# Sums of log decays over chunks as 64-row blocks in the two row halves of the TensorE array

## The chip, the cores and the metric

The kernel runs on one core of a Trainium2 chip. The metric is the device time of one execution in microseconds (us). The time before the change is 1380.78 us, the median of three runs (1379.42 to 1381.92).

## The reference

Two layers of a trunk with four parallel branches run over 128 context tokens and 512 latent tokens. One branch is an RWKV-7 mixer with a forward and a backward scan, and its decays are what the change touches:

```python
wd_t = jnp.tanh(wd.astype(jnp.float32))
for d, rev in ((0, False), (1, True)):
    w_log = -jax.nn.softplus(-(lp['rw_w0'][d] + wd_t @ lp['rw_w_up'][d])) - 0.5
    decay = heads(jnp.exp(-jnp.exp(w_log)))
    ...
    s_fin, o = wkv_scan(s_init[:, d], r_h, decay, k_d, v_h, kk, a, rev)
```

Inside the scan every step computes `S = S * w_t - sa * (kk_t * a_t) + v_t * k_t` and reads out `S r_t`. The other branches are a chunk mixer, an attention (windowed for the latent tokens) and a pooling mixer; all are gated, projected up, merged and projected out.

## The kernel before

All 640 tokens (T) are held as columns, in two halves of 320 (HF). The large products are taken with 128x128 weights from HBM, each split into a high and a low part in a reduced fp32 format, so that a product is three matmuls over 320 columns: `hi,whi`, `lo,whi`, `hi,wlo`, written to a PSUM tile `m`. These are called mains here. They come in a fixed order and run almost without a break.

Everything else is side work, in Python generators that the class `Clock` weaves between the mains. `Clock` keeps a table of modelled costs and times, and at each `yield` of the main stream it decides whether a side generator's next step is issued. So the order of the instructions on all engines is settled when the program is written, and a change in one step's shape can move later steps. The matmuls of a step stand together, as an island between mains. Small results go to two PSUM banks `x` that are handed out in turn by `X()`; a step that takes a bank waits until its earlier contents have been read.

The scan of the mixer works on chunks of 64 tokens (C; NC = 10 of them) with plain fp32 matmuls, which the trace shows as two records each. `scan(ft, ...)` runs once for each half of the features (ft 0 and 1), and in it `decay(d)` once for each direction, in both layers: eight times in all. `decay` has three steps. The first makes the rates `th` and `kd`; the second computes `s1`, the log decays, as 128 tokens by 128 features in five tiles; the third sums `s1` along each chunk. For the sum `s1[:, tt, :]` (128 tokens, so two chunks) is the stationary operand, loaded as weights, and the constant `tri0` or `tri1` (128x128) is the moving one. `tri0` is zero outside its two diagonal blocks of 64, and `tri1` outside its two off-diagonal ones, so that a token meets only its own chunk (in `tri1` the two chunks change places, as the backward scan runs from the end). The sums go through two exponentials on ScalarE, to `w` and `wi`, which `keys(d)` multiplies into `kb` and `qr` on VectorE.

In the trace `s1`, `w` and `wi` are parts of a tile named A, the constants are `cst`, and the matmuls of the third step read `x<-cst,A`. In the attention of the latent tokens, `x<-xm` and `c<-y,xm` are matmuls; `x<-qr,kb` belongs to the scan and `x<-cst,xm` is a transpose of the chunk mixer. All matmuls have line 332, all transposes line 336, all ScalarE, VectorE and GpSimd work line 291, where helpers issue them.

Of the kernel before, what the change touches and what calls it, by code (L numbers as in the profile page):

```python
# [11 lines left out]
AF = mybir.ActivationFunctionType  # L12
ALU = mybir.AluOpType

P = 128
# [5 lines left out]
T = TP + TS  # L21
HF = T // 2
C = 64
NC = T // C
DECAY = -0.5 * math.exp(-0.5)
# [271 lines left out]
def hybrid_layers_kernel(ctx: ExitStack, tc: tile.TileContext, xt, cond, condb, wm, wt, wa, wb, wo, pa, pb, pc, gfin, kctx, vctx,  # L297
# [16 lines left out]
    def X():  # L314
        return ck.alloc("x", ps_x.tile([P, 512], F32, tag="x", name="x"), 2)
# [8 lines left out]
    V, A, G, PE = Engine(nc.vector, "V", ck), Engine(nc.scalar, "A", ck), Engine(nc.gpsimd, "G", ck), nc.tensor  # L324
# [5 lines left out]
    def mm(out, lhsT, rhs, start=True, stop=True):  # L330
        ck.matmul(out, lhsT, rhs, 1 if rhs.dtype == F32R else 4)
        PE.matmul(out, lhsT, rhs, start=start, stop=stop)  # L332
# [8 lines left out]
    def K(n):  # L341
        o = CST_AT[n]
        return c_sb[:, o:o + (2 if n == "sel" else P)]
# [330 lines left out]
    def layer(l, h, prb):  # L674
# [23 lines left out]
        def scan(ft, ta, kt, rt, vt):  # L698
            kk, th = ta[:, 1], ta[:, 3]
            tb = S([P, 4, T], "A1")  # L700
            kd, w, wi, s1f = (tb[:, i] for i in range(4))
            s1 = s1f.rearrange("p (n c) -> p n c", c=P)
# [7 lines left out]
            def decay(d):  # L710
                pxs = [X(), X()]
                for b, px in enumerate(pxs):
                    mm(px[:, 0:HF], ap[ROWS[b], d, ft * P:(ft + 1) * P], adt[ROWS[b], hs[b]])
                for b, px in enumerate(pxs):
                    A.activation(th[:, hs[b]], px[:, 0:HF], AF.Tanh, bias=a0h[:, 2 * d + ft:2 * d + ft + 1], scale=0.5)
                    A.activation(kd[:, hs[b]], th[:, hs[b]], AF.Identity, bias=kab[:, ft:ft + 1],
                                 scale=kah[:, ft:ft + 1])
                    A.activation(th[:, hs[b]], th[:, hs[b]], AF.Identity, bias=eps[:, 3:4], scale=0.5)
                yield
                for t0, n in ((0, 4), (4, 1)):  # L720
                    px = X()
                    for i in range(n):
                        tt = t0 + i
                        mm(px[:, P * i:P * i + P], wdt[0:65, tt * P:(tt + 1) * P], wup[0:65, ft, d])
                    A.activation(s1[:, t0:t0 + n], px[:, 0:P * n].rearrange("p (n c) -> p n c", n=n), AF.Tanh, scale=0.5)
                    V.tensor_scalar(s1[:, t0:t0 + n], s1[:, t0:t0 + n], 1.0, None, ALU.add)
                yield
                for t0, n in ((0, 1), (1, 4)):
                    px = X()
                    for i in range(n):  # L730
                        tt = t0 + i if d == 0 else t0 + n - 1 - i
                        mm(px[:, i * P:(i + 1) * P], s1[:, tt, :], K(f"tri{d}"))
                    sl = slice(t0 * P, (t0 + n) * P)
                    if d:
                        sl = slice(T - (t0 + n) * P, T - t0 * P)
                    A.activation(w[:, sl], px[:, 0:n * P], AF.Exp, scale=DECAY)
                    A.activation(wi[:, sl], px[:, 0:n * P], AF.Exp, scale=-DECAY)

            def keys(d):
                dn = slice(NC * d, NC * d + NC)  # L740
# [20 lines left out]
                else:  # L761
                    V.tensor_tensor(bon, bon, kd, ALU.add)
                    V.scalar_tensor_tensor(bon, bon, prm("rk")[:, ft:ft + 1], rt, ALU.mult, ALU.mult)

            yield from decay(0)
            yield f"{L}k{ft}"
            n2 = []
# [7 lines left out]
            for b in range(2):  # L775
                px = X()
# [12 lines left out]
            for d in range(2):  # L789
                for c0, n in ((0, 8), (8, 2)):  # L790
                    px = X()
                    for hh in range(2):
                        r = slice(64 * hh, 64 * hh + 64)
                        if d:
                            mm(px[r, 0:n * C], K("anti")[r, r], vn[hh][r, c0:c0 + n, :].rearrange("p c s -> p (c s)"))
                            continue
                        for i in range(n):
                            mm(px[r, i * C:(i + 1) * C], vt[r, (c0 + i) * C:(c0 + i + 1) * C], K("ident")[r, r])
                    for hh in range(2):
                        r = slice(64 * hh, 64 * hh + 64)  # L800
                        src = px[r, 0:n * C].rearrange("p (c s) -> p c s", s=C)
                        o0 = 2 * NC - c0 - n if d else c0
                        A.copy(vn[hh][r, o0:o0 + n, :], src[:, ::-1, :] if d else src)
                yield
                yield from keys(d)
                if d == 0:
                    yield from decay(1)
                    yield
            yield
            for b in range(2):  # L810
                px = X()
# [6 lines left out]
            for c0 in range(0, 2 * NC, 4):  # L818
                px = [X(), X()]
                for i in range(4):  # L820
                    for hh in range(2):
                        r = slice(64 * hh, 64 * hh + 64)
# [13 lines left out]
            for c0 in range(0, 2 * NC, 4):  # L836
                px = X()
# [39 lines left out]
            px = [X(), X()]  # L877
# [10 lines left out]
            px = [X(), X()]  # L888
# [805 lines left out]
```

## Time and profile before

| | |
|---|---|
| median of 3 runs | 1380.78 us |
| the profiled execution, its own time | 1381.1 us |
| its span, first to last instruction | 1379.3 us |
| granted TensorE clock, mean | 0.995 |
| TensorE matmuls busy | 1339.5 us (97%) |
| VectorE busy | 926.0 us (67%) |
| ScalarE busy | 565.7 us (41%) |

The time outside the span is 1.8 us. Busy time is the union of the records of an engine. A matmul's record lasts longer than the interval to the next one, because matmuls are pipelined; what a matmul costs is read from start to start.

### The profile page before, as it was taken

What the parts mean: (1) busy time and instruction counts of PE and PEld (TensorE: products, weight loads), DVE (VectorE), ACT (ScalarE), POOL (GpSimd) and SP (SyncE); (2) the same over time, 40 slices, a digit from 0 to 9 for tenths busy, and PEclk for the clock granted to TensorE, in tenths of its full rate; (3) what the DMA queues carried; (4) which work ended last, traced back from release to release, by engine and by line L of the source; (5) the groups of instructions that cost most, each with busy time, mean ns of one, the idle gap of its engine ahead of it and who ended that gap; (6) DMA issues with size and microseconds to landing.
All of it is one profiled execution on the core that took longest, in us unless ns stands there. A gap on an engine that the chain in (4) does not pass through costs nothing.

```text
span 1379.3 us, 27713 instructions
## 1 busy us (share of the span) xinstructions
PE 1339.5 (97%) x11350; PEld 1253.4 (91%) x11350; DVE 926.0 (67%) x2056; ACT 565.7 (41%) x1258; POOL 51.8 (4%) x43
## 2 busy tenths in 40 slices
PE   5999999999999999999999999999999999999997
PEld 3898889988999988999989988899899999899997
DVE  5767778755777865658887767694378585463475
ACT  5456532234532333325554555223354233242364
POOL 0100010000000000000001001100001000000000
PEclk9999999999999999999999999999999999999998
DMA  9421134421224342741223121423122333144012
GB/s 373 142 84 39 62 94 123 108 76 58 68 73 130 108 105 62 259 177 63 76 78 118 62 70 59 106 84 82 32 67 59 89 85 89 38 153 155 22 39 77
DMA packets 86504, 132.61 MB, mean 96 GB/s; under 512 B 44744, under 2 KB 46152, under 8 KB 84456
## 3 DMA queue, kind: packets, MB, share of 16 engines
q1 hardware_dynamic: 86376, 130.84, 30.6%
q8 instruction: 89, 1.46, 0.4%
q14 instruction: 39, 0.32, 0.1%
HBM read 120.46 MB, written 10.35 MB: 95 GB/s over the span
## 4 chain that ended last, share of the span: by engine, by line
PE 83%; issue 6%; DVE 5%; ACT 3%; DMA 1%; POOL 1%; SPq 0%; POOLq 0%; DVEq 0%; ACTq 0%
PE m L332 65%; PE x L332 9%; PE c L332 5%; PE o L332 2%; DVE wlo L291 2%; DVE t L291 1%; ACT whi L291 1%; PE x L336 1%; DMA qr<-wm 1%; PE o L336 1%; DMA xm<-xt 1%; PE c L336 0%; ACT vn L291 0%; DVE kb L291 0%; ACT hi L291 0%
## 5 line engine op out<-in xcount | busy, mean ns | idle before, releaser
L332 PE MATMUL m<-hi,whi 128*128 128x320 f32 x2064 | 664.5, 322 | 3.1 <-ACT whi L291 1.6
L332 PE MATMUL m<-hi,wlo 128*128 128x320 f32 x2064 | 638.7, 309 | 2.8 <-DVE wlo L291 2.8
L332 PE MATMUL m<-lo,whi 128*128 128x320 f32 x2064 | 637.8, 309 | 2.0 <-DVE lo L291 1.3
L332 PEld LDWEIGHTS m<-hi,whi 128*128 128x128 f32 x2064 | 387.7, 188 | 25.6 <-issue 9.9
L332 PEld LDWEIGHTS m<-lo,whi 128*128 128x128 f32 x2064 | 388.2, 188 | 5.1 <-DVE lo L291 2.0
L332 PEld LDWEIGHTS m<-hi,wlo 128*128 128x128 f32 x2064 | 387.6, 188 | 5.6 <-DVE wlo L291 5.6
L291 ACT CAST whi<-raw 128x640 fp32r<-128x640 f32 (+1 forms) x220 | 148.9, 681 | 264.1 <-PE m L332 247.1
L291 DVE TENSOR_TENSOR wlo<-raw,whi 128x640 fp32r<-128x640 f32 (+1 forms) x220 | 171.8, 784 | 106.2 <-ACT whi L291 102.4
L291 ACT ACTIVATE t<-m 128x320 f32<-128x320 f32 x152 | 64.6, 436 | 91.8 <-PE m L332 91.6
L291 DVE SCALAR_TENSOR_TENSOR t<-t,m 128x320 f32<-128x320 f32 x120 | 57.9, 482 | 53.6 <-PE m L332 44.0
L291 DVE TENSOR_TENSOR kb<-kb 80x31 f32<-80x31 f32 (+15 forms) x248 | 84.7, 342 | 11.3 <-DMA kb<-ad 4.6
L332 PE MATMUL m<-ysh,whi 128*128 128x320 f32 x256 | 82.5, 322 | 0.0
L332 PE MATMUL m<-ysh,wlo 128*128 128x320 f32 x256 | 79.1, 309 | 0.0
L332 PE MATMUL m<-ysl,whi 128*128 128x320 f32 x256 | 78.9, 308 | 0.0
L291 DVE CUSTOM_DVE_ANT_0 junk<-wt,sil 128x1024 bf16<-128x1024 f32 x64 | 77.9, 1217 | 0.8 <-DMA wt<-wt 0.8
L291 DVE TENSOR_TENSOR xm<-xm,t 128x320 f32<-128x320 f32 x96 | 49.6, 517 | 3.3
L332 PEld LDWEIGHTS m<-ysh,whi 128*128 128x128 f32 x256 | 48.1, 188 | 2.5 <-issue 0.6
L332 PEld LDWEIGHTS m<-ysl,whi 128*128 128x128 f32 x256 | 48.1, 188 | 0.1
L332 PEld LDWEIGHTS m<-ysh,wlo 128*128 128x128 f32 x256 | 48.1, 188 | 0.0
L291 ACT ACTIVATE vn<-c 64x128 f32<-64x128 f32 x40 | 10.9, 272 | 85.7 <-DVE vn L291 85.7
L291 DVE RECIPROCAL t<-t 128x320 f32<-128x320 f32 x16 | 34.4, 2149 | 10.9 <-ACT t L291 10.9
L291 DVE CUSTOM_DVE_ANT_0 kbt<-x,xm 128x512 f32<-128x512 f32 (+3 forms) x56 | 26.8, 516 | 19.7 <-PE x L332 19.7
(242 smaller groups left out, 1512.4 us busy)
## 6 DMA issues: line engine op xcount, KB each, us to landing
raw<-wb SPq DMA_DIRECT2D x128, 320.0 KB
raw<-wa SPq DMA_DIRECT2D x92, 256.0 KB
wt<-wt SPq DMA_DIRECT2D x32, 512.0 KB
A<-wm SPq DMA_DIRECT2D x4, 1024.0 KB
A<-wo SPq DMA_DIRECT2D x8, 512.0 KB
xm<-xt SPq DMA_DIRECT2D x4, 640.0 KB
ad<-A SPq DMA_DIRECT2D x8, 320.0 KB
qr<-wm SPq DMA_DIRECT2D x2, 1024.0 KB
```

What stands on the lines that cost most here:

```text
L291: return f(out, *a, **k)
L332: PE.matmul(out, lhsT, rhs, start=start, stop=stop)
L336: PE.transpose(out, in_, K("ident"))
```

## The change

The third step of `decay` takes each half of 64 tokens by itself. Matmuls `(tt, rb)` use rows 0 to 63 (rb 0) or 64 to 127 (rb 1) of `s1[:, tt, :]` and only the 64x64 block of `tri` that is not zero. So ten matmuls with 64 rows, 128 weight columns and 64 moving columns stand where five with 128, 128 and 128 stood. They alternate between the row halves. The two halves write to different banks: one bank collects the even chunks, the other the odd ones, five blocks of 64 columns each. Both banks are taken at the start. The four exponentials cover 320 columns each (one bank, five blocks), written to every other block of 64 in `w` or `wi`; before, two covered 128 columns and two 512, and the first pair needed only the first matmul.

```diff
-                for t0, n in ((0, 1), (1, 4)):
-                    px = X()
-                    for i in range(n):
-                        tt = t0 + i if d == 0 else t0 + n - 1 - i
-                        mm(px[:, i * P:(i + 1) * P], s1[:, tt, :], K(f"tri{d}"))
-                    sl = slice(t0 * P, (t0 + n) * P)
-                    if d:
-                        sl = slice(T - (t0 + n) * P, T - t0 * P)
-                    A.activation(w[:, sl], px[:, 0:n * P], AF.Exp, scale=DECAY)
-                    A.activation(wi[:, sl], px[:, 0:n * P], AF.Exp, scale=-DECAY)
+                px = [X(), X()]
+                for tt in range(NC // 2):
+                    for rb in range(2):
+                        r = slice(C * rb, C * rb + C)
+                        n, blk = (4 - tt, 1 - rb) if d else (tt, rb)
+                        mm(px[blk][:, n * C:n * C + C], s1[r, tt, :], K(f"tri{d}")[r, C * blk:C * blk + C])
+                for x, scale in ((w, DECAY), (wi, -DECAY)):
+                    for blk in range(2):
+                        A.activation(x.rearrange("p (n b c) -> p b n c", b=2, c=C)[:, blk],
+                                     px[blk][:, 0:HF].rearrange("p (n c) -> p n c", c=C), AF.Exp, scale=scale)
```

What stands on TensorE at the first of the eight sums (layer 0, ft 0, forward), before:

```order
L332 MATMUL m<-hi_250,whi 128x320
L332 MATMUL m<-lo_251,whi 128x320
L332 MATMUL m<-hi_250,wlo 128x320
L332 MATMUL x<-cst,A_870 128x128 x5
L332 MATMUL m<-hi_248,whi 128x320
L332 MATMUL m<-lo_249,whi 128x320
L332 MATMUL m<-hi_248,wlo 128x320
```

The same place after:

```order
L332 MATMUL m<-hi_250,whi 128x320
L332 MATMUL m<-lo_251,whi 128x320
L332 MATMUL m<-hi_250,wlo 128x320
L332 MATMUL x<-cst,A_870 128x64 x10
L332 MATMUL m<-hi_248,whi 128x320
L332 MATMUL m<-lo_249,whi 128x320
L332 MATMUL m<-hi_248,wlo 128x320
```

Here nothing moves: ten smaller matmuls stand between the same mains. From here on the order of the side work differs in places. The next island, `x<-xm`, follows after 12 mains where it followed after nine; in the scan of layer 0, ft 0, later islands stand some 20 to 60 mains further back, and from its end on the two kernels run much alike. The islands between mains are 269 where they were 271.

One such place is the first transpose of the chunk mixer's values in layer 0 (`x<-cst,xm`), which takes both banks `x`. Before, it follows transposes of `kb`:

```order
L332 MATMUL m<-hi_248,whi 128x320
L332 MATMUL m<-lo_249,whi 128x320
L332 MATMUL m<-hi_248,wlo 128x320
L336 MATMUL x<-cst,kb 128x128 x4
L336 MATMUL x<-cst,xm_2090 128x128 x5
L332 MATMUL m<-hi_250,whi 128x320
```

After, it stands directly behind the fourth of the five `x<-qr,kb` islands, which fill both banks:

```order
L332 MATMUL m<-hi_250,whi 128x320
L332 MATMUL m<-lo_251,whi 128x320
L332 MATMUL m<-hi_250,wlo 128x320
L332 MATMUL x<-qr,kb 128x128 x8
L336 MATMUL x<-cst,xm_2059 128x128 x5
L332 MATMUL m<-hi_248,whi 128x320
```

In layer 1 the two stand so in both kernels.

## Rows read from the trace of the kernel before

**Rows 1.** The page: TensorE's line of part 1, shares of the chain (part 4).

```profile
PE 1339.5 (97%) x11350; PEld 1253.4 (91%) x11350; DVE 926.0 (67%) x2056; ACT 565.7 (41%) x1258; POOL 51.8 (4%) x43
...
PE 83%; issue 6%; DVE 5%; ACT 3%; DMA 1%; POOL 1%; SPq 0%; POOLq 0%; DVEq 0%; ACTq 0%
```

**Rows 2.** Waits of TensorE: total us, times, longest us.

```profile
PE m L332 <- DVE wlo L291: 2.8, 8, 1.0
PE x L336 <- DVE bon L291: 1.7, 1, 1.7
```

**Rows 3.** Timeline of TensorE at the first sum: start, us to the last end.

```profile
92.16 0.31 PE L332 MATMUL m<-lo,whi 128*128 128x320 f32 x1
92.30 0.31 PE L332 MATMUL m<-hi,wlo 128*128 128x320 f32 x1
92.45 1.27 PE L332 MATMUL x<-cst,A 128*128 128x128 f32 x10
93.48 0.39 PE L332 MATMUL m<-hi,whi 128*128 128x320 f32 x1
93.71 0.31 PE L332 MATMUL m<-lo,whi 128*128 128x320 f32 x1
93.85 0.31 PE L332 MATMUL m<-hi,wlo 128*128 128x320 f32 x1
```

**Rows 4.** Timeline at the first of the islands `x<-qr,kb` (64 rows each).

```profile
179.36 0.31 PE L332 MATMUL m<-hi,wlo 128*128 128x320 f32 x1
179.59 1.16 PE L332 MATMUL x<-qr,kb 64*128 64x128 f32 x16
180.69 0.41 PE L332 MATMUL m<-hi,whi 128*128 128x320 f32 x1
180.94 0.31 PE L332 MATMUL m<-lo,whi 128*128 128x320 f32 x1
```

**Rows 5.** Timeline where two moving columns meet 128 weight columns.

```profile
671.19 0.72 PE L332 MATMUL x<-cst,nacc 128*128 128x2 f32 x6
671.78 0.81 PE L332 MATMUL x<-cst,t 128*128 128x2 f32 x6
672.45 0.39 PE L332 MATMUL m<-hi,whi 128*128 128x320 f32 x1
```

**Rows 6.** Timeline where 64 moving columns meet 64 weight columns, in pairs.

```profile
284.09 0.69 PE L332 MATMUL c<-vn,kbt 128*64 128x64 f32 x16 [0.25 <-ACT vn L291]
284.60 0.64 PE L332 MATMUL o<-A,vn 128*64 128x64 f32 x16
```

**Rows 7.** Weight loads grouped by form: count, busy us, mean ns, idle before.

```profile
L332 PEld LDWEIGHTS x<-qr,kb 64*128 64x128 f32 x320 | 19.4, 187 | 3.9 <-issue 2.1 <-DVE t L291 0.6 <-DVE xm L291 0.4
...
L332 PEld LDWEIGHTS c<-vn,kbt 128*64 128x64 f32 x288 | 10.7, 137 | 7.5 <-ACT vn L291 3.9 <-issue 3.1 <-ACT t L291 0.6
...
L332 PEld LDWEIGHTS x<-cst,A 128*128 128x128 f32 x80 | 9.8, 191 | 0.2 <-DVE mp L291 0.2
```

**Rows 8.** ScalarE grouped by form: count, busy us, mean ns, idle before.

```profile
L291 ACT ACTIVATE t<-m 128x320 f32<-128x320 f32 x152 | 64.6, 436 | 91.8 <-PE m L332 91.6
...
L291 ACT ACTIVATE A<-x 128x512 f32<-128x512 f32 x24 | 13.5, 598 | 5.8 <-PE x L332 5.8
...
L291 ACT ACTIVATE A<-x 128x128 f32<-128x128 f32 x24 | 5.7, 276 | 2.8 <-PE x L332 2.7
```

**Rows 9.** Timeline of ScalarE at the first sum: its exponentials.

```profile
92.87 0.45 ACT L291 ACTIVATE A<-x 128x128 f32<-128x128 f32 x2 [0.58 <-PE x L332]
93.76 1.09 ACT L291 ACTIVATE A<-x 128x512 f32<-128x512 f32 x2 [0.45 <-PE x L332]
```

**Rows 10.** Timeline of TensorE at `x<-cst,xm`, layer 0 and then layer 1.

```profile
201.32 0.60 PE L336 MATMUL x<-cst,xm 128*128 128x128 f32 x4
202.16 0.33 PE L336 MATMUL x<-cst,xm 128*128 128x128 f32 x1 [0.24 <-ACT kbt L291]
...
861.27 0.83 PE L336 MATMUL x<-cst,xm 128*128 128x128 f32 x5 [0.87 <-DVE A L291]
```

## Prediction

> **What bounds the kernel.** I read the page's first part and the chain before anything else: TensorE is busy 97% of the span, and 83% of the chain that ends last is TensorE's [rows 1]. The reader is to see that ScalarE, VectorE and GpSimd have room, so that a step of theirs costs time only where TensorE waits for it. The list of waits comes next. It shows that such waits are single ones: the group with the most of them has 8, 2.8 us together, and the longest one that is not at the kernel's start or end is 1.7 us [rows 2]. So the time is, to first order, the sum of TensorE's intervals from start to start, and the timeline gives these. From the second main after an island to the third it is 0.14 to 0.15 us (93.71 to 93.85 [rows 3]); this is the pace against which an island is counted.
>
> The granted clock is 0.995 over the span, which is the level of 2.4 GHz nearly throughout. I take no term for it: the mains on both sides stay as dense as they were.
>
> **The change part by part.** One sum before: the last main ahead of it starts at 92.30, the second main behind it at 93.71. That is 1.41 us, two ordinary steps included [rows 3]. Ten records of 128 columns stand in it, 92.45 to 93.48, about 0.10 us each with the way in and out, and there are 80 such records in eight sums [rows 7].
>
> One sum after: ten matmuls of 64 rows, 128 weight columns and 64 moving columns, so 20 records. No such matmul stands in the trace. The nearest row is the scan's own island `x<-qr,kb`: the same 64 rows, the same 128 weight columns, the same alternation of the row halves and of two banks, and only 128 moving columns in place of 64. It takes 0.23 us to get in (179.36 to 179.59), 1.10 us for 16 records to the next main's start (to 180.69), and 0.25 us to the main behind (to 180.94) [rows 4]. The mean over the 16 is 0.069 us, which is below the 0.10 us of a full record: the two halves do run side by side, as eight pairs of records.
>
> The question that decides the sum is what sets the interval between pairs when the moving columns are halved. Two rows stand on either side.
> - If the weights set it, nothing is gained by fewer moving columns. In the island of six records with two moving columns and 128 weight columns the records follow each other at (672.45 - 671.78) / 6 = 0.112 us, though hardly anything moves [rows 5]. And a weight load of 64 rows and 128 columns lasts 187 ns against 191 ns with 128 rows, while one with 64 columns lasts 137 ns [rows 7]: columns count, rows don't.
> - If the moving columns set it, the nearest row is `c<-vn,kbt`, with 64 of both kinds: 16 records from 284.09 to 284.60, eight pairs at 0.064 us each [rows 6].
>
> The new matmuls have the 128 weight columns of the first case, so I take 0.112 us a pair. The island then is that of `x<-qr,kb` with two more pairs: 1.10 + 2 x 0.112 = 1.32 us. From this comes off what the first and the last pair stream without cover, 64 columns less each, at most half a record (0.056 us) apiece; I take half of that, 0.06 us, and so 1.26 us. With the way in and the main behind, 0.23 + 1.26 + 0.25 = 1.74 us against 1.41 us: 0.33 us more a sum, and 8 x 0.33 = 2.6 us in all. The upper end is without the deduction: 1.80 us, 0.39 us more, 3.1 us in all. The lower end is the case of the moving columns: 0.51 + 2 x 0.064 = 0.64 us, and 0.10 us for the way out into another mode (half of the 0.20 us by which 1.10 us exceeds eight pairs at 0.112 us); 0.23 + 0.74 + 0.25 = 1.22 us, 0.19 us less a sum, 1.5 us less in all. The change breaks even where ten pairs come to 0.93 us, which needs an interval of some 0.08 us.
>
> The weight-load rule of the Trainium skill (TensorE: Matmul & The Clock Gate, section "LDWEIGHTS (loading the stationary operand)") says that a load takes the number of weight columns over 1.2 GHz, whatever the number of rows. By it a load of 128 columns is an estimated 107 ns, and the sum would come out near the value taken; the trace's 112 ns agrees. It speaks against this change, which halves rows and moving columns and doubles the loads.
>
> ScalarE: four exponentials of 320 columns replace two of 128 and two of 512. By the grouped rows that is 4 x 436 = 1744 ns against 2 x 276 + 2 x 598 = 1748 ns [rows 8], so no work is added. They start later, though. Before, the first pair started at 92.87, when one matmul was done, and the last ended at 94.85, 2.4 us behind the sum's start at 92.45 [rows 9, 3]. After, nearly all matmuls must be done, so I estimate 1.3 + 1.74 = 3.0 us, 0.6 to 0.7 us later. `keys` on VectorE follows later by as much, and so does the release of both banks. Mains cover it: they don't read `w` or `wi`, and the next user of the banks has been moved to 12 mains behind the sum, where nine were (`x<-xm`). Without the cover it would be 8 x 0.7 = 5.6 us. I take nothing for it.
>
> The moved order: at the first `x<-cst,xm` of layer 0 the transposes now follow `x<-qr,kb` directly and need both of its banks back. Queued behind it are the mains. Where this order already stands, in layer 1, TensorE idles for 0.87 us until VectorE has multiplied the masks in; in layer 0 it idles for 0.24 us at that point today [rows 10]. I take the difference, +0.6 us. Nothing else that I see in the order has a price of its own in a row: the count of islands goes from 271 to 269, and what two switches save is within what the other meetings of islands cost.
>
> Sum: 2.6 + 0.6 = 3.2 us. On the profiled execution, 1381.1 us (its span of 1379.3 us and 1.8 us around it), that is 1384.3 us. The median of the runs is 0.3 us lower, so against it I forecast **1384.0 us**. A measurement of this kernel tells changes from none at about 0.2%, which is 2.8 us: below 1378.0 us is faster, above 1383.5 us slower. The forecast lies only just on the slower side.
>
> **The rivals.**
>
> *Moving columns set the pace.* The row halves load their weights under each other's streaming, and a pair takes the time of 64 columns. For it: `c<-vn,kbt`, where halves of the array alternate at 0.064 us a pair. Against it: its loads are short (137 ns), and the rows with two moving columns stay at 0.112 us. The price is the lower end, -1.5 us, and with the 0.6 us of the moved transpose the time is 1380.8 - 1.5 + 0.6 = 1379.9 us: no change. It decides if the pair interval is below 0.08 us. The Trainium skill (TensorEngine Tiling (Array Packing), section "Theoretical Speedup") gives up to twofold for a contraction of 64 rows or less; halving the 1.03 us between 92.45 and 93.48 would be an estimated 4 us off. No row here shows that gain with 128 weight columns.
>
> *Later exponentials and a new weave make TensorE wait.* In layer 0, where attention, pooling and scan share two banks and VectorE, the new order pushes the scan's steps back by some 20 to 60 mains in places, and each `decay` ends 0.6 to 0.7 us later. For it: most of TensorE's waits are on VectorE or ScalarE. Against it: the mains between are many. Priced at two new waits as long as the longest, 2 x 1.7 = 3.4 us [rows 2]: 1387.4 us. It decides from the first wait that did not stand there before.
>
> *The weave falls out well.* As many of today's waits vanish as VectorE's `wlo` has (2.8 us [rows 2]), and the moved transpose does not wait: 1384.0 - 0.6 - 2.8 = 1380.6 us. For it: these waits depend on small shifts. Against it: most lie where the two layers meet, and the order there is the same in both kernels.
>
> *The halves don't run side by side.* 20 records at 0.112 us, 1.1 us more a sum than forecast: 1384.0 + 8 x 1.1 = 1392.8 us. `x<-qr,kb`, laid out alike, speaks against it.
>
> **How the numbers follow.** The forecast, weights at 0.112 us and little moved, has a chance of 0.58, and its own range is 1381.5 to 1386.5 us. The moving columns get 0.15, the new waits 0.16, the good weave 0.08, halves one after the other 0.03. Slower by over 0.2%: 0.33 of the forecast's 0.58, since its centre is only 0.5 us above the bound, and the 0.16 and 0.03: 0.52. Faster by over 0.2%: 0.03 each from the moving columns and the good weave, where both meet, and 0.01 of the forecast: 0.07. The rest, 0.41, is within 0.2%. The range goes from 1379.2 us, a little below the moving columns, to 1388.2 us, a little above the new waits.
>
> **What the profile after would show.** Right: records `x<-cst,A` with 64 rows and 64 moving columns, 160 of them, in pairs some 0.11 us apart; 1.70 to 1.80 us from the last main ahead of a sum to the second behind it; exponentials of 320 columns near 436 ns; at the first `x<-cst,xm` of layer 0 an idle time near 0.9 us. Wrong: pairs at 0.06 us, a TensorE wait on `w` or `wi` or on what `keys` makes of them, or a changed sum of waits in layer 0 that outweighs 2.6 us.

## The result and the profile after

The changed kernel takes 1392.26 us, the median of four runs (1389.55 to 1394.59), against 1381.35 us (1379.42 to 1382.05) for the kernel before on the same chip: a ratio of 1.0078, with a 95% interval of 1.0064 to 1.0092. It is slower by some 10.9 us, where the forecast of 1384.0 us is 2.6 us above that median, and it lies outside the range. The profiled execution takes 1392.69 us, with a span of 1390.9 us and a mean granted clock of 0.992.

The first part of the page, to be read beside [rows 1]:

```profile
PE 1348.4 (97%) x11430; PEld 1259.5 (91%) x11430; DVE 924.7 (66%) x2056; ACT 565.2 (41%) x1258; POOL 50.6 (4%) x43
```

The reader is to see that TensorE is busy 9 us longer with 80 more matmul records and 80 more weight loads, and that VectorE, ScalarE and GpSimd have no more to do. The timeline of TensorE at the first sum, which answers to [rows 3]:

```profile
93.89 0.31 PE L332 MATMUL m<-hi,wlo 128*128 128x320 f32 x1
94.13 1.33 PE L332 MATMUL x<-cst,A 64*128 64x64 f32 x20
95.39 0.41 PE L332 MATMUL m<-hi,whi 128*128 128x320 f32 x1
95.64 0.31 PE L332 MATMUL m<-lo,whi 128*128 128x320 f32 x1
```

From 93.89 to 95.64 it is 1.75 us, where the forecast had 1.74 us and before stood 1.41 us. So the sums explain at most some 8 x 0.34 = 2.7 us, and 8 us come from elsewhere. The group by form of ScalarE's exponentials, beside [rows 8]:

```profile
L291 ACT ACTIVATE A<-x 128x320 f32<-128x320 f32 x32 | 11.4, 443 | 12.2 <-PE x L332 12.2
```

That is what the prediction took: 443 ns, where it had 436 ns. The waits of TensorE, to be read beside [rows 2] (total us, times, longest us):

```profile
PE x L332 <- DVE t L291: 4.1, 2, 3.0
...
PE x L336 <- DVE A L291: 2.1, 2, 1.3
```

The first line is new in size: one of its two waits for `t` is 3.0 us long. Before, the group reads:

```profile
PE x L332 <- DVE t L291: 1.5, 2, 1.2
```

The place of the new wait is the pooling of layer 1, which the prediction did not look at. The timeline of TensorE there, after the change:

```profile
904.30 0.31 PE L332 MATMUL m<-hi,wlo 128*128 128x320 f32 x1
907.63 1.40 PE L332 MATMUL x<-t,pb 128*128 128x320 f32 x2 [3.02 <-DVE t L291]
908.36 0.93 PE L332 MATMUL m<-hi,whi 128*128 128x320 f32 x1
909.10 0.47 PE L332 MATMUL m<-lo,whi 128*128 128x320 f32 x1
909.36 0.47 PE L332 MATMUL m<-hi,wlo 128*128 128x320 f32 x1
909.63 0.47 PE L332 MATMUL m<-hi,whi 128*128 128x320 f32 x1
...
913.94 0.31 PE L332 MATMUL m<-lo,whi 128*128 128x320 f32 x1
```

The same place in the kernel before:

```profile
901.51 0.31 PE L332 MATMUL m<-hi,wlo 128*128 128x320 f32 x1
902.06 0.78 PE L332 MATMUL x<-t,pb 128*128 128x320 f32 x2 [0.24 <-DVE t L291]
...
905.57 0.30 PE L332 MATMUL m<-lo,whi 128*128 128x320 f32 x1
```

Two things are to be seen: the wait has grown from 0.24 to 3.02 us, and behind it the mains follow each other at 0.265 us (909.10, 909.36, 909.63) where 0.147 us is the pace. From the first `x<-t,pb` to the second main behind the next one (the last line of each) the same matmuls take 6.31 us, where they took 3.51 us. The windows view says why (length; busy us of PE, PEld, DVE, ACT, POOL with their counts; granted clock; DMA share, GB/s):

```profile
core 0: us, PE busy (x) PEld busy (x) DVE busy (x) ACT busy (x) POOL busy (x), PEclk, DMA share, GB/s
899.40:906.90 7.50, 5.21 (x36) 4.94 (x34) 7.22 (x24) 0.73 (x1) 1.65 (x1) 1.00 0.16 44
906.90:913.70 6.80, 6.07 (x20) 5.50 (x20) 6.33 (x15) 0.73 (x1) 0.00 (x0) 0.50 0.20 59
```

From 906.90, still in the wait, the granted clock is 0.50, the level of 1.2 GHz, for 6.8 us. Why `t` is late shows on VectorE. After the change:

```profile
895.07 0.69 DVE L291 TENSOR_TENSOR wlo<-raw,whi 128x512 fp32r<-128x512 f32 x1 [1.38 <-ACT whi L291]
899.10 0.41 DVE L291 TENSOR_TENSOR kb<-kb 80x31 f32<-80x31 f32 x2 [3.34 <-DMA kb<-ad]
899.43 0.86 DVE L291 TENSOR_TENSOR xm<-xm 128x680 f32<-128x680 f32 x1
900.21 3.05 DVE L291 TENSOR_TENSOR kb<-kb 80x60 f32<-80x60 f32 x6
...
906.09 1.39 DVE L291 SCALAR_TENSOR_TENSOR t<-xm 64x128 f32<-64x128 f32 x4
```

And before:

```profile
893.27 0.85 DVE L291 TENSOR_TENSOR xm<-xm 128x680 f32<-128x680 f32 x1
...
896.94 1.47 DVE L291 TENSOR_TENSOR kb<-kb 80x31 f32<-80x31 f32 x6 [0.42 <-DMA kb<-ad]
...
900.52 1.39 DVE L291 SCALAR_TENSOR_TENSOR t<-xm 64x128 f32<-64x128 f32 x4
```

`kb<-kb` are the first operations of the scan's elimination, which has nothing to do with the pooling; their input `kb<-ad` is a transfer that SP issues at 893.05. Before, the pooling's addition over 680 columns stood ahead of them. After, two of them stand ahead of it, VectorE idles 3.34 us for the transfer while the addition stands behind them, and the pooling's chain (`xm`, then GpSimd, then `t`) starts 2.9 us later, counted from an operation that stands ahead of all this in both kernels (`t<-xm`, at 884.46 before and 887.68 after).

The prediction's other place is there as well. The timeline of TensorE at the first `x<-cst,xm` of layer 0, beside [rows 10]:

```profile
198.93 1.16 PE L332 MATMUL x<-qr,kb 64*128 64x128 f32 x16
200.96 0.83 PE L336 MATMUL x<-cst,xm 128*128 128x128 f32 x5 [0.87 <-DVE A L291]
```

In layer 1, where the order is the same in both kernels, the wait at these transposes grew as well, from 0.87 to 1.26 us (the longer of the two in the list's last line).

### The profile page after: what moved, and what is told of

It reads as the page before. It is cut to its first block, busy times and chain, and to the rows that moved or that the text cites. A ratio compares the mean times of both kernels' runs of the same rounds, so it can differ in the third digit from the quotient of the medians.

```text
span 1390.9 us, 27868 instructions
## 1 busy us (share of the span) xinstructions
PE 1348.4 (97%) x11430; PEld 1259.5 (91%) x11430; DVE 924.7 (66%) x2056; ACT 565.2 (41%) x1258; POOL 50.6 (4%) x43
## 5 line engine op out<-in xcount | busy, mean ns | idle before, releaser
L291 ACT ACTIVATE vn<-c 64x128 f32<-64x128 f32 x40 | 10.9, 271 | 82.2 <-DVE vn L291 82.2
L291 DVE TENSOR_TENSOR A<-x,cst 128x512 f32<-128x512 f32 x40 | 25.7, 685 | 22.7 <-PE x L332 22.7
```

What stands on the lines that cost most here:

```text
L291: return f(out, *a, **k)
```

## The experiments

Two theories stood after this. The first: the sums cost what was forecast, and the rest is the order that the planner made of them, above all the one wait of layer 1 and the clock behind it. The second: the new sums cost the whole, through exponentials that end later and hold both banks. The planner can be shown one form of the sums while another is written, so that sums and order can be exchanged.

**Sums of the change, order of before.** The planner's clock is given the old matmuls and exponentials (with `A.dry` set, a ScalarE call is costed and not issued); the new ones are issued past it.

```diff
-                for t0, n in ((0, 1), (1, 4)):
-                    px = X()
+                px = [X(), X()]
+                A.dry = True
+                for j, (t0, n) in enumerate(((0, 1), (1, 4))):
...
-                        mm(px[:, i * P:(i + 1) * P], s1[:, tt, :], K(f"tri{d}"))
+                        ck.matmul(px[j][:, i * P:(i + 1) * P], s1[:, tt, :], K(f"tri{d}"), 4)
...
+                A.dry = False
+                for tt in range(NC // 2):
...
+                        PE.matmul(px[blk][:, n * C:n * C + C], s1[r, tt, :], K(f"tri{d}")[r, C * blk:C * blk + C], start=True, stop=True)
```

> The change's sums, instruction for instruction, in the order of the kernel before: the planner is shown the old sums, so everything around them stands as before. Two theories. First: the eight sums cost 0.33 us each (1.75 us against 1.41 us from the last main ahead to the second main behind), and the rest of the 11 us came from the order that the planner made of them. Then this kernel is 2.6 us above before, about 1384 us (ratio 1.001 to 1.003), `x<-t,pb` of layer 1 waits 0.4 us as before, and the granted clock does not fall to the level of 1.2 GHz there. Second (rival): the new sums themselves cost the 11 us, through exponentials that end later and hold two banks, wherever they stand. Then it is at 1390 to 1393 us (ratio 1.006 to 1.009).

Measured: 1387.29 us, ratio 1.0035 (1.0022 to 1.0048). In the profile six of the eight sums take the 1.75 us again (94.94 to 96.69 at the first); the other two touch another island and grow by 0.15 and 0.35 us, so that the eight come to 2.5 us. There is no wait above 1 us at `x<-t,pb` but the one of 1.2 us that before has too; the granted clock is 1.00 from 902.7 to 912.9. But the clock falls elsewhere, for 3.4 us at 709.5 us. At 0.266 in place of 0.147 us a main, 3.4 us at this level cost 3.4 x (1 - 0.147 / 0.266) = 1.5 us. The sums alone make 4.8 us (3.0 to 6.6) of the 10.9 us, so the second theory falls; the first one's 2.6 us is just below the interval, and the ratio just above the 1.001 to 1.003 expected.

**Sums of before, order of the change.** The same edit the other way round.

> The converse: the sums of the kernel before (80 records of 128 rows, 128 columns, the old exponentials) in the order of the changed kernel. If the order is the cause, it keeps all but the 2.6 us of the sums: 1388.5 to 1390.5 us (ratio 1.005 to 1.007), with VectorE's 3.3 us wait on the transfer kb<-ad ahead of the pooling of layer 1, TensorE's 3 us wait at `x<-t,pb`, and the clock at the level of 1.2 GHz for some 7 us behind it. If the new sums are the cause, it is at 1381 us (ratio 0.999 to 1.001) whatever the order.

Measured: 1392.27 us, ratio 1.0064 (1.0051 to 1.0076). The waits of 3.1 us on VectorE and 2.8 us on TensorE are there, and the clock falls behind them at 910.1 us, for 3.4 us where some 7 us were expected. The ratio is within the one expected, the median above the 1390.5 us given: the old sums in the new order lose most of what the change loses.

**The change, its elimination in layer 1 planned later.**

```diff
                     "h n s t -> (h n) s t"), True, 8)
-            yield
+            yield 3.0 if l == 1 and ft == 0 else None
```

> The changed kernel, but in layer 1 the elimination of the first feature half is planned 3 us later behind its transfer el, so that VectorE has the pooling's 680-column additions ahead of the first operation on kb. TensorE's order is the same but for a neighbouring swap. If that one wait and the fall of the clock behind it made the step of 5.6 us, this kernel is 5 to 6 us below the changed one, 1386 to 1387.5 us (ratio to before 1.0035 to 1.0048), with no wait above 1 us at `x<-t,pb` and no 1.2 GHz near 907 us. If the cause is elsewhere, it stays at 1391 to 1393 us; if only the wait counts and the clock falls anyway, at 1389 to 1390 us.

Measured: 1389.56 us, ratio 1.0046 (1.0033 to 1.0059), against 1.0078 and 1.0081 for the changed kernel. The timeline of VectorE has the addition ahead of `kb<-kb`, `kb<-kb` without a wait, and `t` 3.7 us earlier, though this profile is 1.8 us behind the other one ahead of this place (`t<-xm` at 889.49, where it was 887.68):

```profile
897.48 0.86 DVE L291 TENSOR_TENSOR xm<-xm 128x680 f32<-128x680 f32 x1
...
901.25 0.40 DVE L291 TENSOR_TENSOR kb<-kb 80x31 f32<-80x31 f32 x2
901.57 0.81 DVE L291 TENSOR_TENSOR xm<-xm 64x8 f32<-64x8 f32 x8
902.41 1.39 DVE L291 SCALAR_TENSOR_TENSOR t<-xm 64x128 f32<-64x128 f32 x4
```

TensorE's longest wait for `t` is 1.0 us, and the clock does not fall there. Of the loss 4.4 to 4.8 us are gone: the ratio is within the one expected, the difference a little under the 5 to 6 us. The time alone would also fit the case in which the clock falls anyway (1389 to 1390 us); the profile decides against it.

**The sums in quarters of the array**, in the order of before by the same means: each matmul of the change is split by its weight columns.

```diff
-                        mm(px[blk][:, n * C:n * C + C], s1[r, tt, :], K(f"tri{d}")[r, C * blk:C * blk + C])
+                        for g in (slice(0, C), slice(C, P)):
+                            PE.matmul(px[blk][g, n * C:n * C + C], s1[r, tt, g], K(f"tri{d}")[r, C * blk:C * blk + C], start=True, stop=True)
```

> The order of before, but each sum in quarters of the array: 20 matmuls of 64 rows, 64 weight columns and 64 moving columns (40 records), the exponentials those of the change. It tests what sets the pace: with 128 weight columns a pair of records takes 0.112 us. If loads of 64 columns are what shortens it, four records pass in the time in which quarters stand in the trace now, 0.031 us a record for `c<-rr,A` (16 records, 0.85 us from main to main): 0.85 + 24 x 0.031 = 1.59 us and 0.25 us to the second main, 1.85 us against 1.41 us, 8 x 0.44 = 3.5 us above before, 1385 us. With the 0.049 us a record of `x<-cst,kx` (40 records, 2.30 us from main to main) it is 2.55 us a sum and 9 us above before, 1390 us. A result below before would need less than 0.02 us a record.

Measured: 1382.36 us, ratio 1.0001 (0.9990 to 1.0012). The expectation missed. The timeline of TensorE (the new matmuls are issued past the helper, so their line is 745):

```profile
94.04 0.31 PE L332 MATMUL m<-hi,wlo 128*128 128x320 f32 x1
94.28 0.81 PE L745 MATMUL x<-cst,A 64*64 64x64 f32 x40
95.02 0.41 PE L332 MATMUL m<-hi,whi 128*128 128x320 f32 x1
95.27 0.31 PE L332 MATMUL m<-lo,whi 128*128 128x320 f32 x1
```

From 94.04 to 95.27 it is 1.23 us, 0.18 us less than before and 0.52 us less than the halves. A single record lasts 223 ns by its group, so the 40 start (0.81 - 0.22) / 39 = 0.015 us apart, four in 0.061 us. I had taken the pace from `c<-rr,A`, at 0.031 us a record; those records use two quarters of the array and not four. The gain of 8 x 0.18 = 1.4 us is of the size of the interval and is not shown in the times.

**The kernel before, with that one wait put in.** The old sums; the transfer `kb<-ad` of that place is planned as shorter, so that the two `kb<-kb` stand ahead of the addition.

```diff
-                    "h n s t -> (h n) s t"), True, 8)
+                    "h n s t -> (h n) s t"), True, 1 if l == 1 and ft == 0 else 8)
```

> The kernel before, with its old sums; only the transfer kb<-ad of the first feature half of layer 1 is planned as shorter, so that the first two operations on kb stand ahead of the pooling's 680-column addition on VectorE, as in the changed kernel. The order of VectorE, TensorE (two matmuls `x<-t,pb` some 7 and 16 mains later) and all else up to that point is that of before. If this one wait makes the step, VectorE idles some 2.5 to 3.3 us for kb<-ad and TensorE 1 to 3 us at `x<-t,pb`; with a fall of the granted clock behind it 4 to 6 us above before (ratio 1.003 to 1.0045), without a fall 1 to 3 us (1.001 to 1.002). If such a wait costs nothing in an otherwise unchanged kernel, it is within 0.1% of before, and the new sums are needed for the loss.

Measured: 1385.64 us, ratio 1.0020 (1.0011 to 1.0029). VectorE, then TensorE, then the windows around the fall:

```profile
898.72 0.41 DVE L291 TENSOR_TENSOR kb<-kb 80x31 f32<-80x31 f32 x2 [2.56 <-DMA kb<-ad]
899.05 0.85 DVE L291 TENSOR_TENSOR xm<-xm 128x680 f32<-128x680 f32 x1
```

```profile
907.86 0.92 PE L332 MATMUL x<-t,pb 128*128 128x320 f32 x2 [2.32 <-DVE t L291]
908.23 0.81 PE L332 MATMUL m<-hi,whi 128*128 128x320 f32 x1
```

```profile
903.40:908.40 5.00, 2.68 (x18) 2.35 (x16) 4.72 (x21) 0.73 (x1) 0.00 (x0) 1.00 0.48 131
908.40:911.80 3.40, 3.40 (x14) 3.23 (x13) 3.35 (x9) 0.00 (x0) 0.00 (x0) 0.50 0.22 52
```

Two operations in another order, in a kernel with the old sums, bring a wait of 2.3 us and a fall of the clock behind it: 2.1 us more waiting and 1.5 us for the clock make 3.6 us, and 2.8 us (1.5 to 4.0) are measured, less than the 4 to 6 us expected with a fall. This shows the mechanism without the change.

**The change again, and two variants beside it on one chip.** The changed kernel once more:

> The changed kernel once more, nothing changed, beside its two variants on one chip. Its ratio should come out at 1.0064 to 1.0092. The 3 us wait at `x<-t,pb` of layer 1 should stand in this trace too, since it is set by the order. The fall of the clock near 1350 us, and the rise of the clock in the first 40 us, may stand elsewhere: if they come and go between executions of one kernel, they belong to no part of the change.

Measured: 1394.30 us, ratio 1.0081 (1.0068 to 1.0094). The wait at `x<-t,pb` is there (2.82 us), and the clock falls behind it at 909.8 us, now for 3.4 us. The fall near 1350 us is gone; there is one at 708.4 us instead:

```profile
704.00:708.40 4.40, 3.45 (x27) 3.19 (x26) 3.69 (x8) 2.15 (x5) 0.00 (x0) 1.00 0.27 112
708.40:711.80 3.40, 3.40 (x16) 3.40 (x16) 2.42 (x5) 1.46 (x4) 0.00 (x0) 0.50 1.00 314
```

Then the change's order with the sums in quarters, the wait left in:

> The changed kernel's order with the sums in quarters, the wait of layer 1 left in. By the sums alone: 4.2 us below the changed kernel of this job (ratio to before some 0.003 less than the changed kernel's). The difference to the kernel with both corrections is what the wait and the clock behind it cost, 5 to 6 us by the profiles, 2.5 to 3 us if the clock's part is not lasting.

Measured: 1390.27 us, ratio 1.0045 (1.0033 to 1.0057). That is 0.0036 less than the changed kernel beside it, or 5.0 us, with 4.2 us expected. And with both corrections, quarters and the later elimination:

> Both corrections on the changed kernel's order: the sums in quarters of the array (64 weight columns; 0.98 us from main to main against 1.50 us, so 8 x 0.52 = 4.2 us less), and the elimination of layer 1 planned 3 us later (5.7 us less in the profiles of the run before). If sums and this one wait make up the loss, it stands 8 to 10 us below the changed kernel, within 0.2% of before (ratio 0.999 to 1.002). If a good part of the loss lies elsewhere in the order, it stays at 1.003 or above.

Measured: 1385.75 us, ratio 1.0021 (1.0009 to 1.0033), 8.3 us below the changed kernel and so within the 8 to 10 us expected, but just above the ratio of 1.002 given as its bound. The wait and its clock are worth 0.0024, or 3.3 us, here; 5 to 6 us were expected by the profiles. Each of the two ratios is known to 0.0012, so 5 us is not excluded. It isn't faster than before either: no kernel of this study is.

**Two profiles more**, to see what belongs to an execution.

> The kernel before, one more profile. Its first one had the clock rise to the level of 2.4 GHz at 16.9 us and no fall between 31 us and the end. The profiles of all other kernels, whose first 90 us hold the same instructions, reach the first main 0.8 to 2.9 us later than it. If the start belongs to the execution and not to the kernel, this profile too has the first main 1 to 3 us after 25.6 us, and the span is 1380.5 to 1382.5 us; a single fall of the clock for 3.4 us may stand where TensorE had thin or few matmuls. If it is again at 25.6 us with no fall, the start and the scattered falls belong to the changed kernels.

Measured: 1379.85 us, span 1378.0 us. The expectation missed: the first main is at 25.41 us again, and no clock falls between 31 us and the last 10 us. By the words of the expectation, the later start and the scattered falls then belong to the changed kernels; how far that holds is taken up below.

> The change's sums in the order of before, one more profile: its first one had the sums at 0.33 us each and, beside them, a single fall of the clock near 709.6 us that cost 1.6 us. If that fall belongs to the sums it stands there again; if it belongs to the execution, it is gone or elsewhere, and from the 150th main to the end this profile is 2.5 to 3 us above that of before (1320.0 us).

Measured: 1385.30 us, span 1383.5 us. The fall at 709.5 us is gone; one of 3.4 us at 1344.6 us stands in its place. From the first sum to the end it is 3.7 and 4.9 us above the two profiles of before, 1.5 us of it this fall.

The profiles side by side. The second column is the span less the start of the first sum, so that the start of the kernel is left out; the third is where the clock fell to 0.50 between 60 us and the last 12 us of the span (for 3.4 us, once for 6.8 us). Before's first sum starts at 92.45 us [rows 3]. The kernels of the first eight experiments were profiled on another chip than before's second profile; only their ratios compare runs of one chip.

| kernel | ratio of the times | first sum to end, us | falls of the clock at, us |
|---|---|---|---|
| before, two profiles | 1 | 1286.9, 1285.7 | none; none |
| new sums, old order, two profiles | 1.0035 | 1290.3, 1290.6 | 709.5; 1344.6 |
| quarters, old order | 1.0001 | 1285.6 | none |
| before with `kb<-kb` early | 1.0020 | 1289.9 | 908.4 |
| changed kernel, two profiles | 1.0078, 1.0081 | 1296.8, 1295.4 | 906.9 (6.8 us), 1350.6; 708.4, 909.8 |
| old sums, new order | 1.0064 | 1296.4 | 285.4, 910.1, 1350.4 |
| quarters, new order | 1.0045 | 1296.0 | 494.9, 907.9, 1348.2 |
| change, elimination later | 1.0046 | 1291.6 | 646.5 |
| quarters, new order, later | 1.0021 | 1288.9 | 945.4 |

All four kernels with `kb<-kb` ahead of the addition have a fall at 907 to 910 us, in five profiles of five. None of the five without it has one there, in seven profiles. This includes both directions: the old sums with the wait put in have the fall, and the change with the wait taken out has not.

## Why the prediction was wrong

**The sums: right.** 0.33 us each were forecast, 0.34 us measured. The pairs go at the pace that the weights set: (1.33 - 0.28) / 19 = 0.055 us a record, 0.11 us a pair (277 ns is the mean of one record of `x<-cst,A`), where 0.112 us was taken. With 64 weight columns in quarters, a round of four takes 0.061 us for the same 64 moving columns; so it is the weight columns and not the moving ones, and the first rival is out. Its 2.6 us are the part of the forecast that came. In the old order the two profiles of the new sums are 3.4 to 4.9 us above before's two from the first sum on; 1.5 us of it is the one fall that each has, which leaves 1.9 to 3.4 us.

**ScalarE: right in the main.** The four exponentials of the first sum end at 96.91 us, 2.8 us behind the sum's start at 94.13, where I had 3.0 us:

```profile
95.49 1.42 ACT L291 ACTIVATE A<-x 128x320 f32<-128x320 f32 x4 [1.61 <-PE x L332]
```

With the new sums in the old order, no group in the list of TensorE's waits is longer than before, but for one at the kernel's start (`shift`, 1.6 us against 0.7 us, in its first profile); the mains covered the delay.

**The moved transpose: right.** 0.87 us of idle time at `x<-cst,xm` in layer 0 against 0.24 us, +0.63 us, and +0.6 us was taken. The 0.4 us more at the same transposes of layer 1 were not foreseen.

**The order elsewhere: wrong, and this is the step that failed.** I wrote that nothing else in the order "has a price of its own in a row", the rival of new waits looked at layer 0 alone, and the description of the change has the two kernels run much alike behind the first scan. On VectorE they don't: in the pooling of layer 1, the new order carries two VectorE operations ahead of another one. Their price could be read: before, their input `kb<-ad` lands only at 896.94 us, where its first user still waits 0.42 us for it, and that is 3.7 us behind the start of the addition at 893.27 us. Put ahead of the addition, they had to wait some 3.6 us by this row; 3.34 us were measured. So the rival named the right mechanism in the wrong layer, as two waits of 1.7 us; it was one of 3.02 us, 2.8 us more than before.

**The clock: wrong.** I took no term for it, because the mains stay dense on both sides. Behind this wait they don't: 6.1 of the 6.8 us at 0.50 fall on matmuls, nearly all of them mains (906.90 to 913.70 less the wait until 907.63), which cost an estimated 6.1 x (1 - 0.147 / 0.266) = 2.7 us, as much as the wait. The same matmuls read in both kernels give 6.31 - 3.51 = 2.8 us. The fall at 1350.6 us cost 1.5 us more.

The terms for the changed kernel's first profile: sums 2.7, wait 2.8, clock behind it 2.7, second fall 1.5, moved transpose 0.6, together 10.3 us. From first sum to end it lost 9.9 or 11.1 us, by which profile of before is taken. For its second profile they are 2.7, 2.6, 1.5, 1.5 and 0.6, together 8.9 us, where 8.5 or 9.7 us were lost. The later start comes on top of this: the first sum starts at 94.13 us where it started at 92.45, which is 1.7 us of the 11.6 us between the two spans and stands in no term.

**What stays open.** The scattered falls change place between executions of one kernel (709.5 or 1344.6 us; 1350.6 or 708.4 us), so none of them is bound to one instruction of the change. Of the ten in the table, six stand at two places, 708 to 710 us and 1344 to 1351 us, and three right behind gaps of over 1 us in TensorE's work that the last section shows. Before had none in two profiles, and each of the eight profiles with the halves or the new order had at least one. But two profiles are few: of the 40 other runs of before that stand beside the experiments, seven have a mean granted clock of 0.992 or 0.993, as low as in the two profiles of the new sums in the old order (0.993), and take 1384.7 us in the median, where the 17 runs at 0.995 take 1381.9 us. In which part of these runs the clock was low is not known. So the part of the loss that is due to the scattered falls, some 1.5 us each, is argued, not shown; what keeps the kernel with both corrections at 1.0021 is open in the same way.

The start is open too: the first main was at 25.4 and 25.6 us in both profiles of before and at 26.3 to 28.5 us in the ten others, among them the kernel that differs from before only near 900 us. The change cannot be the cause there; what is, no run shows.

## What to carry to other kernels

A matmul cut into row halves keeps its number of weight columns, and where these set the pace, halving the rest doubles the records for nothing; look for a row with the same weight columns before counting on it. Where a planner sets the order, go through the whole difference of every engine, and ask of each operation that moved ahead when its input lands: here two that came before their transfer held up VectorE, and all that was queued behind them, for 3.34 us. And price a wait of some microseconds on a dense TensorE with the stretch at half clock that follows it.

## What the runs showed of the hardware

A wait of 2.3 to 3.0 us in an otherwise dense stretch was followed by the level of 1.2 GHz for 3.4 or 6.8 us in each of the five profiles that had it; one place so cost 3.6 us (before with `kb<-kb` early) to 5.5 us (the changed kernel) by the profiles, and 2.8 to 4.8 us by the times of the three pairs of kernels that differ in it. Shorter waits went by without it: the one of 1.7 us for `bon` [rows 2] stands in all twelve profiles, and none has a fall behind it.

The quarters were the other surprise: 40 records of 64 rows, 64 weight columns and 64 moving columns in 0.74 us (94.28 to 95.02), where 20 records of twice the weight columns took 1.26 us (94.13 to 95.39). The Trainium skill (TensorEngine Tiling (Array Packing), section "Theoretical Speedup") gives up to twofold for one dimension of 64 or less. With 128 weight columns this case shows none of it: the sum grew from 1.41 to 1.75 us. Only with rows and weight columns both at 64 is it shorter than before, 1.23 us.

Three profiles with the new order show TensorE idle for over 1 us inside the many `x<-A,v` matmuls of 32 rows without anything that the waits view could name. Here it is in the kernel with both corrections, ahead of its fall of the clock at 945.4 us:

```profile
942.69 1.38 PE L332 MATMUL x<-A,v 32*32 32x32 f32 x74
945.28 0.35 PE L332 MATMUL x<-A,v 32*32 32x32 f32 x6 [1.21 <-issue]
```

The others are the old sums in the new order (2.0 us until 283.64 us, a fall at 285.4 us) and the quarters in it (1.7 us until 493.86 us, a fall at 494.9 us). No run was made on the cause of these gaps, but the transfers in the traces point to one. The page of the changed kernel lists two queues of instructions; this is the larger one (packets, MB, share):

```profile
q8 instruction: 89, 1.46, 0.4%
```

That is one transfer of 16 KB for 257 of TensorE's 22860 records of matmuls and weight loads. The twelve profiles have seven such gaps behind the first 45 us, of 0.24 to 2.03 us, all in the new order and all in `x<-A,v`; each ended 1.25 to 1.40 us after a transfer of this queue had landed. At the gap shown, 74 matmul records had passed in 1.38 us ahead of the gap. So TensorE most likely ran out of instructions there; that is read from the timing alone and tested by no run.
